# A chunked RWKV recurrence: products on half arrays instead of block diagonals, old state added on TensorE, two groups half a step apart

## The chip, the cores and the metric

The kernel runs on one core of one Trainium2 chip. The metric is the device time of one execution in microseconds, the median of several runs. All times below come from the timed runs or from one execution taken by the hardware profiler.

## What is computed

A trunk of two layers over 1024 tokens and width 1024: attention and feed-forward, then an RWKV-7 time mix and feed-forward, all in 32-bit floats. The part at issue is the time mix's recurrence for 16 heads of 64, cut here to what matters:

```python
def wkv7_scan(r, decay, k, v, a_vec, b_vec):
    def step(state, inp):
        r_t, w_t, k_t, v_t, a_t, b_t = inp
        sa = jnp.einsum('bhvk,bhk->bhv', state, a_t)
        state = state * w_t[:, :, None, :] + sa[..., None] * b_t[:, :, None, :] + v_t[..., None] * k_t[:, :, None, :]
        return state, jnp.einsum('bhvk,bhk->bhv', state, r_t)
    _, ys = lax.scan(step, state0, xs)
...
    y = wkv7_scan(rh, decay, kh, vh, -kk, kk * ah)
    y = ((y - mean) * lax.rsqrt(var + LNX_EPS)).reshape(bsz, s, dm) * lnx_w + lnx_b
    y = y + bonus.reshape(bsz, s, dm)
    out = (y.astype(h.dtype) * g) @ w_o
```

## The kernel before

The time steps are taken in 16 chunks of 64 tokens, a chunk being a step `c` of the stage `rwkv_scan`. Everything that doesn't depend on the state is made beforehand by `rwkv_dense` and kept in DRAM: per chunk and head, the matrices `nk` (64x64), `ar` (64x128: one half for the right side, one for the output), `km` and `bm` (64x128: one half for the new state, one for the output), and `u`, the inverse of a triangular matrix. Its diagonal blocks of 32 come from `solve`: 62 VectorE operations (L1076, L1077) for a quarter of the heads and chunks at a time, four times. The off-diagonal block of each 64 is made in `inverse`, for a pair of chunks at a time, by two rounds of eight TensorE products (L1406, L1414), with ScalarE copies from u (L1410), of tb (L1411) and back into u (L1417) between and behind them.

The 16 heads lie as 8 head pairs, one head in each half of the 128 partitions, and these in 2 groups of 4. A step does for each group, in `step`:

- `o1` = nk x vb + ar x S (L1477, L1479, L1483). Two heads of a pair share one product; the right operands `vb` and `S` are block diagonals, zero outside, so that 128 columns are streamed for two times 64 useful ones.
- `rb`, the right side, copied out of PSUM into a block diagonal in two halves, one by ScalarE (L1485), one by VectorE (L1486).
- `z` = u x rb (L1489), copied into the block diagonal `sb` in the same way (L1490, L1491).
- `o2` = km x vb + bm x sb (L1493, L1495): new state and output.
- the state: VectorE adds the old state (`se`, L1503), GpSimd multiplies by the decay `el` (`S`, L1504).
- the output `y`: a ScalarE copy of the rest of o1 (L1510) and a VectorE addition (L1511).

After each odd step the pair of chunks is finished (`finish`): mean on VectorE (L1520, L1521), y - mean on GpSimd (L1522), the square on ScalarE (L1524), variance on VectorE (L1525, L181), the power -1/2 (L183) and two products on GpSimd (L1530, L1531), y + vn on VectorE (L1532), transposes on TensorE (L1537), the gate on VectorE (`yg`, L1540), and a split into two parts for the output projection: a ScalarE cast and a VectorE subtraction (L154).

Loads of a step (`load`) go through SyncE's queue into two sets of buffers, by the parity of the step; `u` is loaded for two steps at once (`load2`). Each engine works through its own rows strictly in the order in which the built program has them, and waits on semaphores for the others. The order of the rows is made when the program is built, by a scheduler that goes by its own estimates of the durations; `chained` fixes the order of some matmuls. The last solve is called as `last()` after the second step.

Of the kernel before, what the change touches and what calls it, by code (L numbers as in the profile page):

```python
# [1028 lines left out]
def rwkv_dense(t, hp, sv, hT, first):  # L1029
# [73 lines left out]
    for q in range(2):  # L1103
# [156 lines left out]
        for c in range(NK):  # L1260
# [55 lines left out]

            tm = [tp.tile([P, 8, P], F32, name="tm", tag="tm") for _ in range(2)]
            for e in range(2):
                rows = slice(e * 64, e * 64 + 64)
                na = tp.tile([P, 8, 64], F32, name="na", tag="na")  # L1320
                for h in range(2):
                    h4 = slice(h * 4, h * 4 + 4)
                    ps = pg.tile([P, 4, P], F32, name="pg", tag="pg")
                    for i in range(4):
                        pe.matmul(ps[:, i], bk[rows, h * 4 + i].rearrange("p x t -> p (x t)"),  # L1325
                                  ar[rows, h * 4 + i].rearrange("p y t -> p (y t)"), start=True, stop=True)
                    mask = lambda y: mg[:, y * 64:y * 64 + 64].unsqueeze(1).broadcast_to([P, 4, 64])
                    ve.tensor_tensor(na[:, h4], ps[:, :, 0:64], mask(0), MUL)
                    ve.tensor_tensor(tm[e][:, h4, 64:], ps[:, :, 64:], mask(1), MUL)
                nc.sync.dma_start(d["n"][q, e, :, c], na[0:64])  # L1330
                nc.sync.dma_start(d["nk"][cs, rows, c].rearrange("c p t -> p c t"), na[64:])

            for h in range(2):
                h4 = slice(h * 4, h * 4 + 4)
                ps = pg.tile([P, 4, P], F32, name="pg", tag="pg")
                for i in range(4):
                    pe.transpose(ps[:, i], bk[:, h * 4 + i].rearrange("p x t -> p (x t)"), t.ident)
                for e in range(2):
                    ac.copy(tm[e][:, h4, 0:64], ps[:, :, e * 64:e * 64 + 64])
# [21 lines left out]
class Scan:  # L1361


    def __init__(self, t, d):
# [5 lines left out]
        self.zs = [(self.zeroed(lp, "nk0", 1, 2, 5, 64)[0], self.zeroed(lp, "vb0", 1, 2, 8, 64)[0])]  # L1370
# [11 lines left out]

    def more(self, sp):
        self.pools.append(sp)
        self.zs.append((self.zeroed(sp, "nk1", 1, 2, 5, 64)[0], self.zeroed(sp, "vb1", 1, 2, 8, 64)[0]))
# [33 lines left out]
    def load(self, c):  # L1419
        nc, d, pool = self.t.nc, self.d, self.pools[c % 2]  # L1420
        r = []
        for n in ("ar", "bm", "km"):
            x = pool.tile([P, 8, P], F32, name=n, tag=n)
            nc.sync.dma_start(x, d[n][c])
            r.append(x)
        nk, vb = self.zs[c % 2]
        nc.sync.dma_start(nk[:, :, 0:4], d["nk"][c].rearrange("p (g k) t -> p g k t", g=2))
        for e in range(2):
            nc.sync.dma_start(vb[self.half[e], e], d["v"][e, c * 64:c * 64 + 64])
        self.tiles[c % 2] = r + [nk, vb]  # L1430


def rwkv_scan(t, d, ld, sv, last):
# [11 lines left out]
    p1, pz, p2, pq, pg = (pool(n, b, space=PSUM) for n, b in (("sp1", 2), ("spz", 2), ("sp2", 2), ("spq", 1), ("spg", 1)))  # L1445
    Ss, rbs, sbs = (ld.zeroed(sp, n, m, 4, P) for n, m in (("S", 4), ("rb", 2), ("sb", 2)))
    ld.more(sp)
    lo, hi = half = [slice(0, 64), slice(64, P)]

    def chained(seq):  # L1450

        prev = None
        for f in seq:
            ins = f()
            if prev is not None:
                tc.add_manual_dep(ins.ins, prev.ins.name,
                                  mybir.DependencyInfo(mybir.DependencyClass.NoSync, mybir.DependencyReason.DATA), reason="order")
            prev = ins
# [9 lines left out]
    def step(c, two, ar, bm, km, nk, vb):  # L1468
        cc = c % 2
        us, y = two  # L1470
        for grp in range(2):
            pairs = list(enumerate(range(4 * grp, 4 * grp + 4)))
            S, S2, rb, sb = Ss[2 * grp + cc], Ss[2 * grp + 1 - cc], rbs[grp], sbs[grp]
            o1 = p1.tile([P, 4, P], F32, name="o1", tag="o1")
            nkf = nk[:, grp].rearrange("p k t -> p (k t)")

            seq = [lambda: pe.matmul(o1[:, 3], nkf[:, 192:320], vb[:, :, 4 * grp + 3], start=True, stop=c == 0, skip_group_check=True)]  # L1477
            for i, k in pairs[:3]:
                seq.append(lambda i=i, k=k: pe.matmul(o1[lo, i], nk[:, grp, i], vb[:, :, k], start=False, stop=c == 0,  # L1479
                                                      skip_group_check=True))  # L1480
            if c:
                for i, k in pairs:
                    seq.append(lambda i=i, k=k: pe.matmul(o1[:, i], ar[:, k], S[:, i], start=False, stop=True, skip_group_check=True))  # L1483
            chained(seq)
            ac.copy(rb[lo, :, 0:64], o1[lo, :, 0:64])  # L1485
            ve.tensor_copy(rb[hi, :, 64:], o1[lo, :, 64:])  # L1486
            z = pz.tile([64, 4, P], F32, name="z", tag="z")
            for i, k in pairs:
                pe.matmul(z[:, i], us[cc][:, k], rb[:, i], start=True, stop=True)  # L1489
            ac.copy(sb[lo, :, 0:64], z[:, :, 0:64])  # L1490
            ve.tensor_copy(sb[hi, :, 64:], z[:, :, 64:])  # L1491
            o2 = p2.tile([P, 4, P], F32, name="o2", tag="o2")
            chained([lambda i=i, k=k: pe.matmul(o2[:, i], km[:, k], vb[:, :, k], start=i == 0, stop=False, skip_group_check=True)  # L1493
                     for i, k in pairs] +
                    [lambda i=i, k=k: pe.matmul(o2[:, i], bm[:, k], sb[:, i], start=False, stop=True, skip_group_check=True)  # L1495
                     for i, k in pairs])
            if c + 1 < NC:
                se = tp.tile([P, 4, 64], F32, name=f"se{grp}", tag=f"se{grp}", bufs=1)
                for e in range(2):
                    es_ = slice(e * 64, e * 64 + 64)  # L1500
                    el = d["el"][half[e], 4 * grp:4 * grp + 4, c:c + 1].broadcast_to([64, 4, 64])
                    if c:
                        ve.tensor_tensor(se[half[e]], o2[lo, :, es_], S[half[e], :, es_], ADD)  # L1503
                        po.tensor_tensor(S2[half[e], :, es_], se[half[e]], el, MUL)  # L1504
                    else:
                        ve.tensor_tensor(S2[half[e], :, es_], o2[lo, :, es_], el, MUL)
            ys = y[half[cc], grp * H:(grp + 1) * H].rearrange("p (k x) -> p k x", x=P)
            if c:
                y1 = tp.tile([P, 4, P], F32, name="y1", tag="y1")[half[cc]]
                ac.copy(y1, o1[hi])  # L1510
                ve.tensor_tensor(ys, o2[hi], y1, ADD)  # L1511
            else:
                ve.tensor_copy(ys, o2[hi])
# [36 lines left out]
    prev = None  # L1550
    for c in range(NC):
        here = two
        if c == 0:
# [6 lines left out]
        step(c, here, *ld.tiles[c % 2])  # L1560
# [17 lines left out]

# [53 lines left out]
```

## Time and profile before

| | before |
|---|---|
| median of 3 runs | 2867.52 us (2865.66 to 2872.91) |
| profiled execution | 2867.93 us, its span 2866.2 us |
| mean granted TensorE clock | 0.958 |
| window 1965 to 2098 us (chunk 6 to the end of the recurrence) | 133 us |
| TensorE matmuls / weight loads busy there | 115.5 / 101.3 us |
| VectorE / ScalarE / GpSimd busy there | 86.1 / 55.1 / 79.0 us |
| granted clock, DMA share, rate there | 0.97, 0.70, 196 GB/s |

How to read the rows in the next parts. A row of the windows has the stretch, its length, the busy time of PE (matmul), PEld (weight load), DVE (VectorE), ACT (ScalarE) and POOL (GpSimd), then granted clock, DMA share and GB/s. A row of the groups has line, engine, operation, out<-in, shapes and count, then busy time and mean ns of one, then the engine's idle time just before them and what ended it. Rows of the chain of waits and of the timeline begin with the start time and the duration; SPq is SyncE's queue. Matmul ends are modelled. A matmul in 32-bit floats is two records.

### The profile page before, as it was taken

To read this page: it belongs to the slowest core of one execution; us is meant where nothing else is said; L and a number is where in the kernel's file an instruction comes from. 1 tells how busy PE (TensorE), PEld (TensorE's weight loads), DVE (VectorE), ACT (ScalarE), POOL (GpSimd) and SP (SyncE) were. 2 spreads that over 40 slices of the span, in tenths; PEclk is the share of its full clock that TensorE was granted. 3 is DMA by queue.
4 is the path that set the end of the run, shared out by engine and by line. 5 is a ranking of instruction groups with operands and counts; after the bars stand their busy time and mean duration, and the time that the engine had idled before them with its cause. 6 is when DMAs were issued, how large, how long until landed. Compare 5 with 4: busy or idle time off the path is not lost. (4 is left out here: it accounts for less than half of the span.)

```text
span 2866.2 us, 38024 instructions
## 1 busy us (share of the span) xinstructions
PE 2674.2 (93%) x13302; PEld 2135.3 (75%) x13302; DVE 1789.1 (62%) x3017; ACT 1204.6 (42%) x2377; POOL 1099.7 (38%) x830
## 2 busy tenths in 40 slices
PE   8999997799999999998899889888899999999998
PEld 6777775577888877786577667777787888887776
DVE  4555555457444437798667888767676544444988
ACT  3445444234333334355544454434334433333334
POOL 1221211136443424545444433334643534431644
PEclk9999997799999999999999999789999999999999
DMA  4111111452222227462446366787743222225654
GB/s 138 38 45 46 45 51 46 150 191 78 83 82 78 85 94 263 151 207 78 154 138 166 98 212 163 195 216 208 208 162 129 89 89 77 85 70 184 217 155 162
DMA packets 301536, 367.18 MB, mean 128 GB/s; under 512 B 101000, under 2 KB 175112, under 8 KB 301344
## 3 DMA queue, kind: packets, MB, share of 16 engines
q1 hardware_dynamic: 296560, 351.08, 39.5%
q10 hardware_dynamic: 4496, 12.62, 1.1%
q8 instruction: 105, 1.72, 0.3%
q0 software_dynamic: 288, 1.05, 0.1%
q14 instruction: 87, 0.71, 0.1%
HBM read 268.98 MB, written 95.68 MB: 127 GB/s over the span
## 5 line engine op out<-in xcount | busy, mean ns | idle before, releaser
L910 PE MATMUL pd<-ws,as 128*128 128x512 f32 x1848 | 435.7, 397 | 19.9 <-DVE ws L154 18.8
L910 PEld LDWEIGHTS pd<-ws,as 128*128 128x128 f32 x1848 | 353.5, 192 | 100.0 <-DVE ws L154 23.9
L762 PE MATMUL y<-t,cw 128*128 128x512 f32 x1584 | 370.2, 389 | 0.0
L762 PEld LDWEIGHTS y<-t,cw 128*128 128x128 f32 x1584 | 297.3, 188 | 62.4
L154 DVE TENSOR_TENSOR cw<-raw,cw 128x512 fp32r<-128x512 f32 x264 | 214.5, 815 | 197.2 <-ACT cw L154 195.9
L154 ACT CAST cw<-raw 128x512 fp32r<-128x512 f32 x264 | 163.4, 621 | 242.5 <-PE z L762 102.3
L154 ACT CAST wh<-raw 128x512 fp32r<-128x512 f32 (+1 forms) x154 | 119.8, 780 | 202.5 <-PE mm L174 58.4
L154 DVE TENSOR_TENSOR wl<-raw,wh 128x512 fp32r<-128x512 f32 (+1 forms) x146 | 144.0, 988 | 95.2 <-ACT wh L154 94.9
L771 POOL TENSOR_TENSOR c<-c 128x512 f32<-128x512 f32 x66 | 111.4, 1688 | 188.1 <-DVE c L778 137.0
L173 PE MATMUL mm<-hx,wh 128*128 128x512 f32 x384 | 163.3, 425 | 0.0
L766 ACT COPY sn<-y 128x512 f32<-128x512 f32 x132 | 77.0, 588 | 196.4 <-PE y L762 193.1
L175 PE MATMUL mm<-hx,wl 128*128 128x512 f32 x384 | 152.3, 397 | 0.0
L174 PE MATMUL mm<-hx,wh 128*128 128x512 f32 x384 | 151.6, 395 | 0.0
L762 PE MATMUL z<-b,cw 128*128 128x512 f32 x576 | 141.6, 396 | 6.6 <-DVE tx L708 6.6
L257 POOL TENSOR_TENSOR ry<-ry,S 128x512 f32<-128x512 f32 x40 | 52.0, 1301 | 222.5 <-DVE ry L256 198.0
L154 ACT CAST as<-raw 128x512 fp32r<-128x512 f32 x110 | 68.3, 621 | 157.4 <-PE pd L910 82.3
L762 PEld LDWEIGHTS z<-b,cw 128*128 128x128 f32 x576 | 110.2, 192 | 30.8 <-issue 7.0
L762 PE MATMUL y<-b,cw 128*128 128x512 f32 x528 | 129.0, 394 | 0.0
L762 PE MATMUL z<-t,cw 128*128 128x512 f32 x528 | 123.3, 389 | 0.0
L804 POOL TENSOR_TENSOR raw<-s,raw 128x512 f32<-128x512 f32 x44 | 59.9, 1362 | 152.8 <-DVE cw L154 152.6
L762 PE MATMUL x<-b,cw 128*128 128x512 f32 x480 | 117.4, 400 | 0.0
L154 DVE TENSOR_TENSOR as<-raw,as 128x512 fp32r<-128x512 f32 x110 | 100.0, 909 | 27.4 <-ACT as L154 27.3
(469 smaller groups left out, 6122.5 us busy)
## 6 DMA issues: line engine op xcount, KB each, us to landing
raw<-act SPq DMA_DIRECT2D x132, 256.0 KB, 3.5
raw<-in_wd SPq DMA_DIRECT2D x132, 256.0 KB, 3.3
raw<-in_wg SPq DMA_DIRECT2D x88, 256.0 KB, 2.9
raw<-in_wu SPq DMA_DIRECT2D x88, 256.0 KB, 2.5
act<-c SPq DMA_DIRECT2D x88, 256.0 KB, 2.0
raw<-in_wrk SPq DMA_DIRECT2D x32, 512.0 KB, 4.6
raw<-in_win SPq DMA_DIRECT2D x24, 512.0 KB, 3.3
raw<-in_wout SPq DMA_DIRECT2D x32, 256.0 KB, 3.8
```

Source lines behind the costliest of these rows:

```text
L154: return self.nc.scalar.copy(hi, src), (eng or self.nc.vector).tensor_tensor(lo, src, hi.bitcast(F32), SUB)
L173: seen(mm(ps, lh, rh, start=start, stop=False))
L174: seen(mm(ps, lh, rl, start=False, stop=False))
L175: seen(mm(ps, ll, rh, start=False, stop=stop))
L257: nc.gpsimd.tensor_tensor(y, y, self.S[:, s], MUL)
L762: seen(pe.matmul(ps, w[:, x, s], bs[:, k, y], start=start and k == j == 0, stop=k == 3 and j == 2, skip_group_check=True))
L766: ac.copy(s, ps)
L771: po.tensor_tensor(g, g, u, MUL)
L804: po.tensor_tensor(a11, s, a11, SUB)
L910: pe(ps[b], s[:, x, t], w[:, y], start=first and i == 0, stop=f == N - 1 and i == 2, skip_group_check=True)
```

## The change

Each head gets its own products. A head's operands lie in one half of the partitions, so that a product with 64x64 weights uses a quarter of TensorE's array, and one with 64 rows and 128 columns of weights a half; the heads of a pair alternate. Per group and step these are 8 products nk x v and 8 ar x S into the first half of one PSUM tile `xz`, 16 for the old state (the identity times S into the state's half of o2, and the output half of ar times S into the other), 8 km x v, 8 u x rb into the second half of `xz`, and 8 bm x sb. `o2` is now two PSUM tiles, one for each head of a pair. The block diagonals, their zeroing, `se`, `y1` and GpSimd's part are gone: `rb` is one ScalarE copy, `sb` one VectorE copy, the state two VectorE products with the decay, the output two ScalarE copies. In DRAM, the halves of `km` and `bm` of the second head are swapped. The loads come in the order ar, nk, vb, km, bm, with the same bytes. All products of the recurrence are chained in the order of the code, and the two groups, now generators, are advanced in turn, so that group 1 is half a step behind group 0.

The core of the diff:

```diff
@@ load
-        for n in ("ar", "bm", "km"):
-            x = pool.tile([P, 8, P], F32, name=n, tag=n)
-            nc.sync.dma_start(x, d[n][c])
...
+        ar = pool.tile([P, 8, P], F32, name="ar", tag="ar")
+        nc.sync.dma_start(ar, d["ar"][c])
+        nk, vb = (pool.tile([P, 8, 64], F32, name=n, tag=n) for n in ("nk", "vb"))
...
@@ rwkv_scan
-    p1, pz, p2, pq, pg = (pool(n, b, space=PSUM) for n, b in (("sp1", 2), ("spz", 2), ("sp2", 2), ("spq", 1), ("spg", 1)))
-    Ss, rbs, sbs = (ld.zeroed(sp, n, m, 4, P) for n, m in (("S", 4), ("rb", 2), ("sb", 2)))
+    p1, p2, pq, pg = (pool(n, b, space=PSUM) for n, b in (("sp1", 2), ("sp2", 4), ("spq", 1), ("spg", 1)))
...
+    def mm(*x, **k):
+        ins = pe.matmul(*x, **k, skip_group_check=True)
+        if order:
+            t.after(ins, order.pop())
+        order.append(ins)
...
-    def step(c, two, ar, bm, km, nk, vb):
...
+    def group(g):
+        Ss, S = [sp.tile([P, 4, 64], F32, name=f"S{g}{i}") for i in range(2)], None
+        both = [(i, e, half[e]) for i in range(4) for e in range(2)]
+        k0 = 4 * g
+        for c in range(NC):
+            us, y = here
+            ar, bm, km, nk, vb = ld.tiles[c % 2]
+            xz = p1.tile([P, 2, 4, 64], F32, name="xz", tag="xz")
+            for i, e, r in both:
+                mm(xz[r, 0, i], nk[r, k0 + i], vb[r, k0 + i], start=i == 0, stop=c == 0)
+            if c:
+                for i, e, r in both:
+                    mm(xz[r, 0, i], ar[r, k0 + i, 0:64], S[r, i], start=False, stop=True)
+            rb, sb = (tp.tile([P, 4, 64], F32, name=n, tag=f"{n}{g}", bufs=1) for n in ("rb", "sb"))
+            ac.copy(rb, xz[:, 0])
+            yield
+            o2 = [p2.tile([P, 4, 64], F32, name="o2", tag="o2") for _ in range(2)]
+            if c:
+                for i, e, r in both:
+                    mm(o2[e][r, i], t.ident[r, r], S[r, i], start=i == 0, stop=False)
+                    mm(o2[e][half[1 - e], i], ar[r, k0 + i, 64:], S[r, i], start=i == 0, stop=False)
+            for i, e, r in both:
+                mm(o2[e][:, i], km[r, k0 + i], vb[r, k0 + i], start=c == i == 0, stop=False)
+            for i, e, r in both:
+                mm(xz[r, 1, i], us[c % 2][r, k0 + i], rb[r, i], start=True, stop=True)
+            ve.tensor_copy(sb, xz[:, 1])
+            yield
+            for i, e, r in both:
+                mm(o2[e][:, i], bm[r, k0 + i], sb[r, i], start=False, stop=True)
+            if c + 1 < NC:
+                S = Ss[c % 2]
+                for e, r in enumerate(half):
+                    ve.tensor_tensor(S[r], o2[e][r], d["el"][r, k0:k0 + 4, c:c + 1].broadcast_to([64, 4, 64]), MUL)
+            ys = y[half[c % 2], g * H:(g + 1) * H].rearrange("p (k e v) -> p e k v", e=2, v=64)
+            for e in range(2):
+                ac.copy(ys[:, e], o2[e][half[1 - e]])
+            yield
...
+    groups = [group(g) for g in range(2)]
     for c in range(NC):
         here = two
+        next(groups[0])
+        if c:
+            next(groups[1])
...
-        step(c, here, *ld.tiles[c % 2])
+        next(groups[0])
+        next(groups[1])
+        next(groups[0])
+        next(groups[1])
+        if c + 1 == NC:
+            next(groups[1])
```

The order of the rows around the change moves too. Lines of the changed kernel differ by a few from those of the kernel before; names carry numbers of their buffers.

VectorE, where a pair of chunks ends in the middle of the stage, before (`rb0`, `rb1`, `sb1`, `se0`, `se1` are those of the groups; `mean`, `var` and `rs_v` belong to the finish of the pair that has just ended):

```order
L1520 TENSOR_REDUCE mean_17012<-y_16450 128x16
L154 TENSOR_TENSOR o_15926<-yg_16792,o_15926 128x4x128
L1521 TENSOR_SCALAR mean_17012<-mean_17012 128x16
L1486 COPY rb1_15504<-o1_16859 64x4x64
L1540 SCALAR_TENSOR_TENSOR yg_16804<-pg_16799,vec_62,gt_16572 128x128 x4
L1511 TENSOR_TENSOR y_16691<-o2_16842,y1_16856 64x512
L154 TENSOR_TENSOR o_15927<-yg_16804,o_15927 128x4x128
L1491 COPY sb1_15508<-z_16870 64x4x64
L1486 COPY rb0_15503<-o1_16942 64x4x64
L1525 TENSOR_REDUCE var_17013<-sqy_17017 128x16
L1503 TENSOR_TENSOR se1_16886<-o2_16877,S2_15497 64x256 x2
L1511 TENSOR_TENSOR y_16691<-o2_16877,y1_16891 64x512
```

VectorE at the same place of the changed kernel (`S00` and `S10` are the states of groups 0 and 1 behind the even step; the first `sb` is that of group 0, the second that of group 1):

```order
L154 TENSOR_TENSOR o_16062<-yg_17772,o_16062 128x4x128
L1507 TENSOR_REDUCE mean_18112<-y_17252 128x16
L1508 TENSOR_SCALAR mean_18112<-mean_18112 128x16
L1512 TENSOR_REDUCE var_18113<-sqy_18117 128x16
L181 TENSOR_SCALAR rs_v_18120<-var_18113 128x16
L1489 COPY sb_17801<-xz_17783 128x256
L1496 TENSOR_TENSOR S00_15521<-o2_17826,el_10639 64x256
L1496 TENSOR_TENSOR S00_15521<-o2_17827,el_10639 64x256
L1519 TENSOR_TENSOR y_17252<-y_17252,vn_17779 128x1024
L1489 COPY sb_17879<-xz_17861 128x256
```

Before, the mean and the variance of a finish had other rows between them (eight in this piece), among them copies of rb and sb. Now they follow each other, the first sb copy of the next pair of steps stands behind the variance, and its second sb copy behind `y + vn`.

ScalarE at the same place, before (`u20` is the copy out of the freshly loaded u, `sqy` the finish's square):

```order
L1490 COPY sb0_15507<-z_16835 64x4x64
L1410 COPY u20_13714<-u_16894 32x8x32 x4
L1417 COPY u_16894<-pq_16919 32x8x32 x4
L154 CAST o_15926<-yg_16792 128x4x128
L1485 COPY rb1_15504<-o1_16859 64x4x64
L1510 COPY y1_16891<-o1_16859 64x512
L1411 COPY tb0_13712<-pq_17143 32x8x32 x4
L154 CAST o_15927<-yg_16804 128x4x128
L1490 COPY sb1_15508<-z_16870 64x4x64
L1485 COPY rb0_15503<-o1_16942 64x4x64
L1524 ACTIVATE sqy_17017<-y_16450 128x1024
```

And ScalarE there in the changed kernel (the first `y` row is that of group 0 in the odd step, the two behind the second cast are those of group 1, with which the pair's y is complete):

```order
L1499 COPY y_17252<-o2_17638 64x4x64
L154 CAST o_16061<-yg_17760 128x4x128
L1478 COPY rb_17800<-xz_17783 128x256
L1406 COPY u20_13714<-u_17960 32x8x32 x4
L154 CAST o_16062<-yg_17772 128x4x128
L1499 COPY y_17252<-o2_17704 64x4x64
L1499 COPY y_17252<-o2_17705 64x4x64
L1511 ACTIVATE sqy_18117<-y_17252 128x1024
L1478 COPY rb_17878<-xz_17861 128x256
```

The copies from u, which wait for a load, now stand between the even step's first rb copy and the cast, and ahead of the y copies, of the square and of the second rb copy.

SyncE at the end of the dense stage, before (`n` is what the last solve reads; `n_d`, `bm_d` and `km_d` are in DRAM):

```order
L1342 DMA bm_d_10633<-tm_15403 64x8x128
L1343 DMA km_d_10634<-tm_15403 64x8x128
L1429 DMA vb00_13718<-v_d_10630 64x512
L1565 DMA bo_15729<-bon_d_10631 128x8x16
L1424 DMA bm_15650<-bm_d_10633 128x1024
L1070 DMA n_15731<-n_d_10636 32x32x32 x4
```

And SyncE there in the changed kernel:

```order
L1070 DMA n_15798<-n_d_10636 32x32x32 x2
L1331 DMA n_d_10636<-na_15402 64x512
L1332 DMA nk_d_10635<-na_15402 64x8x64
L1343 DMA bm_d_10633<-tm_15400 64x8x128
L1344 DMA km_d_10634<-tm_15400 64x8x128
L1343 DMA bm_d_10633<-tm_15401 64x8x128
L1344 DMA km_d_10634<-tm_15401 64x8x128
L1070 DMA n_15798<-n_d_10636 32x32x32 x2
```

Two of the solve's four loads have moved ahead of the last stores, and three other issues no longer stand between those stores and the rest. In VectorE's rows, the 62 operations of this solve, which before began behind the sb copies of step 1 and reached to step 5, now begin ahead of the first sb copy of step 0 and end after that of group 0 in step 1.

More of the change, by code (lines that the diff above doesn't have):

```diff
@@ L1328, in rwkv_dense @@
                     ve.tensor_tensor(na[:, h4], ps[:, :, 0:64], mask(0), MUL)
-                    ve.tensor_tensor(tm[e][:, h4, 64:], ps[:, :, 64:], mask(1), MUL)
+                    ve.tensor_tensor(tm[e][:, h4, 64 - 64 * e:P - 64 * e], ps[:, :, 64:], mask(1), MUL)
                 nc.sync.dma_start(d["n"][q, e, :, c], na[0:64])
@@ L1338, in rwkv_dense @@
                 for e in range(2):
-                    ac.copy(tm[e][:, h4, 0:64], ps[:, :, e * 64:e * 64 + 64])
+                    ac.copy(tm[e][:, h4, e * 64:e * 64 + 64], ps[:, :, e * 64:e * 64 + 64])
             for e in range(2):
@@ L1369, in __init__ @@
         self.nb, self.ub, self.tb, self.u2 = (self.zeroed(lp, n, 1, 8, 64)[0] for n in ("nb", "ub", "tb", "u2"))
-        self.zs = [(self.zeroed(lp, "nk0", 1, 2, 5, 64)[0], self.zeroed(lp, "vb0", 1, 2, 8, 64)[0])]
         self.pools, self.us, self.tiles = [lp], [None, None], [None, None]
@@ L1381, in begin @@
         self.load(0)
-    def more(self, sp):
-        self.pools.append(sp)
-        self.zs.append((self.zeroed(sp, "nk1", 1, 2, 5, 64)[0], self.zeroed(sp, "vb1", 1, 2, 8, 64)[0]))
     def load2(self, g):
@@ L1420, in load @@
         nc, d, pool = self.t.nc, self.d, self.pools[c % 2]
-        r = []
-        for n in ("ar", "bm", "km"):
-            x = pool.tile([P, 8, P], F32, name=n, tag=n)
-            nc.sync.dma_start(x, d[n][c])
-            r.append(x)
-        nk, vb = self.zs[c % 2]
-        nc.sync.dma_start(nk[:, :, 0:4], d["nk"][c].rearrange("p (g k) t -> p g k t", g=2))
-        for e in range(2):
-            nc.sync.dma_start(vb[self.half[e], e], d["v"][e, c * 64:c * 64 + 64])
-        self.tiles[c % 2] = r + [nk, vb]
+        ar = pool.tile([P, 8, P], F32, name="ar", tag="ar")
+        nc.sync.dma_start(ar, d["ar"][c])
+        nk, vb = (pool.tile([P, 8, 64], F32, name=n, tag=n) for n in ("nk", "vb"))
+        nc.sync.dma_start(nk, d["nk"][c])
+        for e in range(2):
+            nc.sync.dma_start(vb[self.half[e]], d["v"][e, c * 64:c * 64 + 64])
+        km, bm = (pool.tile([P, 8, P], F32, name=n, tag=n) for n in ("km", "bm"))
+        nc.sync.dma_start(km, d["km"][c])
+        nc.sync.dma_start(bm, d["bm"][c])
+        self.tiles[c % 2] = ar, bm, km, nk, vb
 def rwkv_scan(t, d, ld, sv, last):
@@ L1444, in rwkv_scan @@
     sp, tp = pool("ss", 1), pool("st", 2)
-    p1, pz, p2, pq, pg = (pool(n, b, space=PSUM) for n, b in (("sp1", 2), ("spz", 2), ("sp2", 2), ("spq", 1), ("spg", 1)))
-    Ss, rbs, sbs = (ld.zeroed(sp, n, m, 4, P) for n, m in (("S", 4), ("rb", 2), ("sb", 2)))
-    ld.more(sp)
+    p1, p2, pq, pg = (pool(n, b, space=PSUM) for n, b in (("sp1", 2), ("sp2", 4), ("spq", 1), ("spg", 1)))
+    ld.pools.append(sp)
     lo, hi = half = [slice(0, 64), slice(64, P)]
[L1450 to L1458, printed above, removed]
+    order = []
+    def mm(*x, **k):
[3 more added lines that the diff above has]
+        order.append(ins)
     def load3(g):
@@ L1466, in load3 @@
         return vn, gt
-    def step(c, two, ar, bm, km, nk, vb):
[L1469 to L1480, printed above, removed]
-            if c:
[L1482 to L1496, printed above, removed]
-            if c + 1 < NC:
[L1498 to L1513, printed above, removed]
```

## The prediction, on record before the run

> **What bounds the kernel now.** I read the page first, then the table of windows to find the stage that the change touches, the groups of that stage, its waits, and the chain of waits in order of time. The recurrence over the 16 chunks runs from about 1865 to 2098 us, and it is not a stage of full TensorE: in the window 1965 to 2098 (chunk 6 to the end) TensorE is busy in 115.5 of 133 us, VectorE in 86.1, GpSimd in 79.0, and the DMA engines in 0.70 of the time.
>
> ```profile
> 1965.00:2098.00 133.00, 115.53 (x927) 101.32 (x926) 86.11 (x171) 55.08 (x123) 78.97 (x63) 0.97 0.70 196
> L1486 DVE COPY rb<-o 64x256 f32<-64x256 f32 x19 | 7.9, 416 | 15.1 <-ACT rb L1485 14.8
> L1504 POOL TENSOR_TENSOR S<-se,el 64x256 f32<-64x256 f32 x38 | 25.7, 675 | 26.1 <-DVE se L1503 24.5
> L1491 DVE COPY sb<-z 64x256 f32<-64x256 f32 x20 | 8.3, 417 | 5.5 <-ACT sb L1490 5.1
> L1485 ACT COPY rb<-o 64x256 f32<-64x256 f32 x19 | 7.0, 366 | 31.9 <-PE o L1483 31.7
> L1410 ACT COPY u<-u 32x256 f32<-32x256 f32 x16 | 6.4, 402 | 15.3 <-DMA u<-u_d 15.1
> L1411 ACT COPY tb<-pq 32x256 f32<-32x256 f32 x16 | 5.8, 362 | 2.7 <-PE pq L1406 2.5
> L154 ACT CAST o<-yg 128x512 fp32r<-128x512 f32 x12 | 7.3, 618 | 1.4 <-DVE yg L1540 1.3
> ```
>
> Nineteen copies of rb at two a step are 9.5 steps in 133 us, so a step takes 14.0 us and a pair of steps 28.0. The reader is to see two things: the pieces of work are small (0.4 us copies, 0.7 us state products), and engines mostly wait for one another. One wait to keep in mind is ScalarE's for the load of u.
>
> ```profile
> 1979.28 1.12 PE pq L1406 x16
> ...
> 1981.48 0.89 PE o L1495 x8
> 1982.38 1.02 PE z L1489 x8
> 1983.39 0.93 PE pq L1414 x16
> 1984.74 0.80 PE o L1479 x6
> ...
> 1994.33 5.52 DMA u<-u_d
> ...
> 2020.40 1.10 PE z L1489 x8
> 2021.56 4.35 DMA u<-u_d
> ...
> 2044.31 1.10 PE z L1489 x8
> 2045.47 6.51 DMA u<-u_d
> ...
> 2096.01 2.12 PE o L1495 x16
> ```
>
> In this chain of waits, each matmul is two records. Records that stream 128 columns follow each other every 0.111 us (0.89 over 8), those that stream 64 every 0.058 us (0.93 over 16), and a burst that begins a new shape loses about 0.13 us (1.02 against 0.89; 0.80 for six against 0.67). A load of u starts when the last z that read the buffer has ended, and lands 4.4 to 6.5 us later, 5.5 in the mean. The last product of the recurrence ends at 2098.1.
>
> **TensorE's part of the change.** Per group and step, 20 matmuls (40 records) become 56 (112 records) on half or quarter arrays. Whether halves run at the same time is seen elsewhere in this trace:
>
> ```profile
> 202.53 1.09 PE L490 MATMUL pv<-pT,vt 128*64 128x128 f32 x16
> 205.16 1.13 PE L454 MATMUL sc<-kT,q 64*128 64x256 f32 x8
> 1851.03 2.05 PE L1325 MATMUL pg<-ar,bk 64*128 64x128 f32 x16
> ```
>
> L490 alternates the column halves and takes 1.09 us for sixteen records; L1325, which stays in one row half, takes 2.05 for sixteen of the same length. L454 alternates row halves and takes 1.13 for eight records of 256 columns, which one after another at 0.111 per 128 would be 1.78. So halves overlap. For each of the three products with 64x64 weights (the two into xz, and U with rb) I take 8 x 0.058 = 0.46 us; one after another they would be 0.93. The products with the identity and ar (32 records) lie between 0.46 (four at a time) and 1.86 (none): I take 0.93, pairs, which is what the two rows show. The products with km and bm have 64 moving columns but weights 128 columns wide: between 0.46 and 1.78, I take 0.89, the pace of L454's pairs at 128. With four changes of shape at 0.13, a half-step is 1.39 + 0.93 + 1.78 + 0.52 = 4.6 us, a step 9.2, and with the inverse ((1.12 + 0.93)/2) and the finish's transposes (eight records and two bursts in two steps, 0.6) 10.9 us. If TensorE set the pace, a step would fall from 14.0 to 10.9.
>
> **Why I don't think it sets the pace.** VectorE and ScalarE work through their rows in order, and the rows shown above put the whole finish of a pair (mean, variance, scaling) between the last state product of that pair and the first copies of sb of the next one, back to back. In the kernel before, other work stands between the same links, and they cost almost nothing:
>
> ```profile
> DVE var L1525 <- ACT sqy L1524: 2.9, 1, 2.9
> DVE y L1532 <- POOL y L1531: 1.0, 1, 1.0
> ```
>
> (3.9 us in 133.) What the links take is seen undisturbed at the end of the stage, in the finish of the last pair:
>
> ```profile
> 2098.90 1.22 DVE L1520 TENSOR_REDUCE mean<-y 128x16 f32<-128x1024 f32 x1
> 2101.17 0.17 DVE L1521 TENSOR_SCALAR mean<-mean 128x16 f32<-128x16 f32 x1
> 2101.48 1.91 POOL L1522 TENSOR_TENSOR y<-y,mean 128x1024 f32<-128x1024 f32 x1 [1.95 <-DVE mean L1521]
> 2103.42 1.06 ACT L1524 ACTIVATE sqy<-y 128x1024 f32<-128x1024 f32 x1 [1.86 <-POOL y L1522]
> 2104.51 1.22 DVE L1525 TENSOR_REDUCE var<-sqy 128x16 f32<-128x1024 f32 x1 [0.58 <-ACT sqy L1524]
> 2106.25 0.17 DVE L181 TENSOR_SCALAR rs_v<-var 128x16 f32<-128x16 f32 x1
> 2106.50 2.90 POOL L183 TENSOR_TENSOR rs_r<-rs_v,mhalf 128x16 f32<-128x16 f32 x1 [3.11 <-DVE rs_v L181]
> 2109.47 1.91 POOL L1530 TENSOR_TENSOR y<-y,rs_r 128x1024 f32<-128x1024 f32 x1
> L1531 POOL TENSOR_TENSOR y<-y,lw 128x1024 f32<-128x1024 f32 x5 | 11.8, 2358 | 0.4
> 2114.67 1.21 DVE L1532 TENSOR_TENSOR y<-y,vn 128x1024 f32<-128x1024 f32 x1
> ```
>
> One pair of steps in the changed kernel, from the end of the copy sb (odd step, group 1) round to the same copy:
>
> - A, until the mean may start: ScalarE's four copies from u stand ahead of the cast and of the y copies that the mean needs. The last U product ended 0.77 us earlier (0.35 to VectorE, 0.42 the copy), the load lands 5.5 after that, then four copies of 0.402, a cast of 0.62, two y copies of 0.73 together and 0.3 of hand-overs: 8.0 us. Bounds: 5.3 if u is never late (VectorE's own yg, split and state rows), 9.0 at the longest load.
> - B, the finish from mean to y+vn, which stands ahead of sb (even step, group 1): 1.22 + 0.17 + 1.91 + 1.06 + 1.22 + 0.17 + 2.90 + 1.91 + 2.36 + 1.21 = 14.1, with nine hand-overs 14.6 us. Only one sb copy and one pair of state products fit into its waits.
> - C, three half-steps: sb 0.52; bm 1.0; then 3.5 until the inverse's second half may start (0.25 to VectorE, state 0.84, y copies 0.8, four tb copies of 0.362, hand-overs), that half 1.05, the second half of km 0.57, U 0.58, to VectorE and copy 0.77, bm 1.1, identity, ar and km 2.06, U 0.58, copy 0.77: 12.5 us.
>
> Together 35.1 us for a pair, against 28.0 now. VectorE's saving (the second halves of rb and the additions se and y are gone) and GpSimd's (38 products of 0.675 gone) fall into these waits and bring nothing. The copies of rb and sb in one piece do take 0.8 us out of the round trip; that is in C.
>
> **The clock.** By A and B TensorE then waits about 9 us for the first sb of a pair (mean to rs_v, behind the late y copies) and 4 us for the second (y+vn). After a wait of 2.3 us the trace shows a burst at about half pace:
>
> ```profile
> 1972.66 1.82 PE L1489 MATMUL z<-rb,u 128*64 128x128 f32 x8 [0.45 <-DVE rb L1486]
> ```
>
> (1.82 against 1.02.) Behind the first wait slow products are covered by the finish; behind the second they lie in C. Between 0 and 2 us a pair, I take 1. The Trainium skill (TensorE: Matmul & The Clock Gate, "What's actually happening") says that the array falls to half clock after an idle window of about 3.4 us and recovers after a busy one; by it the second wait would cost an estimated 1.7 us a pair, 12 us in all where I take 7.
>
> **The start.** The fourth triangular solve (62 VectorE operations) is spread over chunks 2 to 6 now, and takes longer beside GpSimd's work than the third did:
>
> ```profile
> 1895.11 0.19 DVE L1076 TENSOR_TENSOR sw<-ub,n 128x31 f32<-128x31 f32 x1 [4.13 <-DMA n<-n_d]
> 1883.89 1.04 SPq L1429 DMA_DIRECT2D vb<-v_d  x1
> 1887.04 4.22 SPq L1070 DMA_DIRECT2D n<-n_d  x4
> L1077 DVE TENSOR_TENSOR ub<-ub,sw 128x31 f32<-128x31 f32 (+15 forms) x31 | 12.7, 411 | 0.6
> L1076 DVE TENSOR_TENSOR sw<-ub,n 128x31 f32<-128x31 f32 (+15 forms) x31 | 11.9, 384 | 1.3 <-DMA n<-n_d 0.9
> ```
>
> In the new order it starts before the first sb copy and ends with one and a half steps done. Three other issues no longer stand ahead of its loads (1887.04 - 1883.89 = 3.2 us), so it starts at about 1892, takes 24.6 (12.7 + 11.9) and carries 3.8 of sb and state rows: 1920.4, and sb (step 1, group 1) ends at 1920.8. From there seven pairs remain: 7 x 35.1 = 245.7, 2 for the last products, 7 for the clock: 2175.5 instead of 2098.1, that is +77 us. What follows the stage is unchanged. The profiled execution took 2867.93 us (the median of the runs is 2867.52), so 2945 us.
>
> **The rivals.**
> - Faster: TensorE sets the pace. Then 1920.8 + 14 x 10.9 + 2 = 2075, 23 us less, 2845. For it speak the falling work of VectorE and GpSimd, and that a 9 us cut of A and B is all that is needed: the change is not slower from a pair of about 26 us down. Against it: GpSimd's links have no slack to give, L1531's five in the stage average 2.36, and the same kind took 1.91 alone; the order of the rows is fixed. 0.07.
> - Halves better than I take them: identity, km and bm all at 0.46. Only C shrinks, by 2 us: 33.1 a pair, +63, 2931. 0.22.
> - The quarter products into xz don't overlap, since both row halves write one bank: no row shows that case, L454 uses two banks. U and the new xz products then cost 0.46 to 0.93 more where they lie in C, about 2 us a pair: 37.1, +91, 2959. The Trainium skill (TensorEngine Tiling (Array Packing), Gotcha 1: PSUM Pressure) states that different row tiles cannot access the same PSUM bank at one time, which is this case; no run here shows it yet. 0.13.
> - The change doesn't do what it says, nothing overlaps: C grows by 6 us, 41.1 a pair, +119, 2987. 0.07.
>
> **How the numbers follow.** My forecast has 0.51; its own range is 2919 (u never late, no clock loss) to 2959. The range of 2900 to 2980 takes in the second and third rival and the bounds of u and the clock, and leaves out the first and the last. A measurement of this kernel can tell about 0.3%, 8.6 us, from no change: faster 0.06, same 0.03, slower 0.91.
>
> **What would show it.** In the profile after, VectorE's variance waits for the square and its y+vn for GpSimd, each some 3 to 5 us in every pair; TensorE's bm products wait for sb; ScalarE's copy from u waits for the DMA; pairs of steps are 35 us apart; the window's DMA share falls to about 0.56 (0.70 x 28.0/35.1). Sixteen 64x64 records should take about 0.5 to 0.6 us. I am wrong if steps come every 11 to 14 us: then something other than the order of VectorE's rows decides.

## The result and the profile after

| | before | after |
|---|---|---|
| median of four runs each, side by side | 2870.22 us (2865.66 to 2875.29) | 2954.24 us (2947.41 to 2957.35) |
| profiled execution, its span | 2867.93, 2866.2 us | 2955.12, 2953.3 us |
| mean granted clock | 0.958 | 0.932 |

The changed kernel is slower: after over before is 1.0292, with a 95% interval of 1.0273 to 1.031. The first view is the table of windows for the recurrence after, from 10 us behind the first sb (odd step, group 1) to just before the last; the columns are those explained above.

```profile
1925.00:2178.00 253.00, 175.20 (x3216) 160.45 (x3216) 82.20 (x174) 69.29 (x170) 74.76 (x34) 0.72 0.47 143
```

TensorE is busy in 69% of the stage (87% before) at a granted clock of 0.72 (0.97 before), and the DMA share fell from 0.70 to 0.47. Per step VectorE, ScalarE and GpSimd are busy for less than before. TensorE is busy for 12.9 us a step (181.0 over 14 steps, 1915.1 to 2178.7 us) where it was 12.2 (115.5 over 9.5), at the lower clock. What grew most is waiting. The waits of the same window (who waits, for whom, us in all, times, longest):

```profile
PEld o L1449 <- DVE sb L1489: 84.1, 14, 15.4
PE o L1449 <- DVE sb L1489: 81.9, 14, 15.3
...
ACT u L1406 <- DMA u<-u_d: 36.3, 6, 10.1
```

All of TensorE's larger waits are for sb copies, fourteen in all: two in each pair of steps. Why sb is late is seen in VectorE's rows of one pair, in order of time (rows of yg, split and state left out):

```profile
2029.22 0.42 DVE L1489 COPY sb<-xz 128x256 f32<-128x256 f32 x1 [1.47 <-issue]
...
2040.91 1.22 DVE L1507 TENSOR_REDUCE mean<-y 128x16 f32<-128x1024 f32 x1
2042.16 0.17 DVE L1508 TENSOR_SCALAR mean<-mean 128x16 f32<-128x16 f32 x1
2045.50 1.22 DVE L1512 TENSOR_REDUCE var<-sqy 128x16 f32<-128x1024 f32 x1 [3.16 <-ACT sqy L1511]
2046.76 0.17 DVE L181 TENSOR_SCALAR rs_v<-var 128x16 f32<-128x16 f32 x1
2046.96 0.42 DVE L1489 COPY sb<-xz 128x256 f32<-128x256 f32 x1
...
2054.36 1.23 DVE L1519 TENSOR_TENSOR y<-y,vn 128x1024 f32<-128x1024 f32 x1 [4.03 <-POOL y L1518]
2055.61 0.42 DVE L1489 COPY sb<-xz 128x256 f32<-128x256 f32 x1
2062.39 0.42 DVE L1489 COPY sb<-xz 128x256 f32<-128x256 f32 x1 [4.28 <-issue]
2066.63 0.42 DVE L1489 COPY sb<-xz 128x256 f32<-128x256 f32 x1 [1.47 <-issue]
```

From 2040.91 to 2055.59 VectorE does one sb copy between the links of the finish: the first copy of the next pair has to let mean and variance by, the second y+vn. From sb to sb this pair took 37.4 us. The chain of waits shows the other half of the story, from the end of this pair into the next:

```profile
2063.22 2.70 PE o L1449 x64
2065.92 0.64 PE xz L1449 x16
...
2066.76 0.59 SPq L1422
...
2067.40 0.58 SPq L1424
...
2068.09 6.64 DMA u<-u_d
2074.75 0.40 ACT u L1406
...
2076.42 0.62 ACT o L154
2077.06 0.37 ACT y L1499
2077.45 0.37 ACT y L1499
2077.84 1.23 DVE mean L1507
...
2083.90 0.44 DVE sb L1489
...
2084.38 4.93 PE o L1449 x64
```

The load of u has to wait for the last U product (it ends at 2066.56), stands behind two other issues in SyncE's queue until 2068.09, and only when it has landed may ScalarE go on to the y copies that the mean needs. The state's products then wait until 2084.38, and take 4.93 us for 64 records, where the same products took 2.70 at 2063.22. That is the clock:

```profile
2072.00:2076.00 4.00, 1.63 (x48) 1.35 (x42) 0.00 (x0) 1.22 (x4) 0.00 (x0) 1.00 1.14 327
2076.00:2084.00 8.00, 0.00 (x0) 0.00 (x0) 3.58 (x6) 3.05 (x6) 1.96 (x2) 0.50 0.15 56
2084.00:2096.00 12.00, 10.66 (x138) 10.01 (x139) 3.66 (x7) 1.54 (x5) 7.10 (x3) 0.50 0.21 65
2096.00:2103.00 7.00, 7.00 (x94) 6.41 (x93) 0.00 (x0) 3.19 (x9) 1.90 (x1) 0.50 1.05 263
2103.00:2108.00 5.00, 5.00 (x118) 4.50 (x116) 1.69 (x4) 1.10 (x3) 0.00 (x0) 0.97 0.44 101
```

The granted clock (third number from the right) is 0.50 behind the wait and stays there for 19 us of nearly unbroken work (one pause of 0.9 us at 2092, for the second sb). At full clock the new products are as fast as hoped; TensorE's rows of the same step once the clock is back:

```profile
2104.05 1.11 PE L1449 MATMUL o<-sb,bm 64*128 64x64 f32 x16
...
2105.71 1.11 PE L1449 MATMUL o<-vb,km 64*128 64x64 f32 x16
2106.75 0.68 PE L1449 MATMUL xz<-rb,u 64*64 64x64 f32 x16
...
2107.95 0.68 PE L1449 MATMUL xz<-vb,nk 64*64 64x64 f32 x16
2108.46 0.63 PE L1449 MATMUL xz<-S,ar 64*64 64x64 f32 x16
```

From start to start, bm with the 32 records of the old state behind it takes 1.66, km 1.04, U 0.61, nk 0.51 and ar 0.57: 4.4 us for a half-step.

### The profile page after: what moved, and what is told of

Read it like the earlier page. It is cut to its first block, busy times and chain, and to the rows that moved or that the text cites. A ratio compares the mean times of both kernels' runs of the same rounds, so it can differ in the third digit from the quotient of the medians.

```text
span 2953.3 us, 42217 instructions
## 1 busy us (share of the span) xinstructions
PE 2684.8 (91%) x15526; PEld 2152.5 (73%) x15526; DVE 1735.2 (59%) x2953; ACT 1197.1 (41%) x2379; POOL 1054.0 (36%) x762
## 5 line engine op out<-in xcount | busy, mean ns | idle before, releaser
L154 DVE TENSOR_TENSOR cw<-raw,cw 128x512 fp32r<-128x512 f32 x264 | 214.3, 814 | 198.1 <-ACT cw L154 197.0
L154 ACT CAST cw<-raw 128x512 fp32r<-128x512 f32 x264 | 163.3, 621 | 243.1 <-PE z L762 102.5
L154 ACT CAST wh<-raw 128x512 fp32r<-128x512 f32 (+1 forms) x154 | 119.6, 779 | 204.6 <-PE mm L174 58.4
L154 DVE TENSOR_TENSOR wl<-raw,wh 128x512 fp32r<-128x512 f32 (+1 forms) x146 | 144.1, 990 | 98.8 <-ACT wh L154 98.5
L1449 PE MATMUL o<-sb,bm 64*128 64x64 f32 x512 | 48.1, 339 | 94.7 <-DVE sb L1489 94.7
L154 ACT CAST as<-raw 128x512 fp32r<-128x512 f32 x110 | 68.2, 620 | 158.1 <-PE pd L910 85.5
L762 PEld LDWEIGHTS y<-b,cw 128*128 128x128 f32 x528 | 98.8, 187 | 22.7
```

The lines of the kernel that those rows point to most:

```text
L154: return self.nc.scalar.copy(hi, src), (eng or self.nc.vector).tensor_tensor(lo, src, hi.bitcast(F32), SUB)
L762: seen(pe.matmul(ps, w[:, x, s], bs[:, k, y], start=start and k == j == 0, stop=k == 3 and j == 2, skip_group_check=True))
L1449: ins = pe.matmul(*x, **k, skip_group_check=True)
```

## The experiments

Two theories stood. **Order**: the products are faster, but VectorE's and ScalarE's rows put the whole finish and the late copy of u into the loop from sb to sb. **TensorE**: the products on half arrays are themselves slow or hinder each other. All ratios below are to the kernel before, run on the same chip beside them (2869.28 to 2870.41 us); differences in us from the changed kernel go by its 2954.24, measured beside 2870.22.

### One cause at a time

`u2`: two buffers for each u, so that its load need not wait for the last product that reads the old one.

```diff
-        u = self.pools[g % 2].tile([P, 8, 2, 64], F32, name="u", tag="u")
+        u = self.pools[g % 2].tile([P, 8, 2, 64], F32, name="u", tag="u", bufs=2)
```

> Only edit: two buffers for each of the two u tiles, so that a load of u needn't wait for the last U product. Theory 'order' (the fixed order of VectorE's and ScalarE's rows puts the finish and the late u on the path of every pair): from the copy sb (odd step, group 1) to the mean falls from about 10.5 us to about 5.3, six times, the finish from mean to y+vn stays at 14.7: about 30 us less than the changed kernel, 2925 us. Rival 'TensorE' (the many small products and the lower clock are the cost): ScalarE's wait goes, the time stays within 9 us of 2954.

Measured: 2918.73 us (2914.93 to 2925.7), ratio 1.0173 (1.0155 to 1.0192), some 35 us better than the changed kernel, near the 2925 of the theory of the order and far from the rival's. The rows of one pair:

```profile
1979.47 0.42 DVE L1489 COPY sb<-xz 128x256 f32<-128x256 f32 x1 [2.23 <-issue]
1985.01 1.22 DVE L1507 TENSOR_REDUCE mean<-y 128x16 f32<-128x1024 f32 x1
...
1998.45 1.23 DVE L1519 TENSOR_TENSOR y<-y,vn 128x1024 f32<-128x1024 f32 x1 [4.04 <-POOL y L1518]
```

From sb's end to the mean it is 5.1 us now (11.3 in the pair shown above); from the mean to the end of y+vn still 14.67. Pairs take 31.3 to 34.1 us instead of 37.4 to 40.9.

`nofin`: the norm and the bonus of the finish are left out (L1507 to L1519; y goes to the transposes as it is).

> The changed kernel without the norm of the finish: mean, y - mean, square, variance, power, the two products and y+vn are left out (and with them the bonus), transposes, gate and split stay; the output isn't the reference's. Products, their number and their shapes are unchanged. Theory 'order': sb no longer stands behind the finish, what is left of a pair is TensorE's 21 us, 2 to 3 us of the late u and 1 to 2 us at the inverse: about 25 instead of 38, seven pairs: 2855 to 2875 us. Rival 'TensorE' (the small products and their clock cost the time): 2930 us or more.

Measured: 2897.81 us (2894.65 to 2900.97), ratio 1.0091 (1.0061 to 1.012): between both theories' numbers, a miss. Pairs take 29.6 to 31.5 us, the granted clock from 1925 to 2075 us is 0.79, and what is left in them is the other cause:

```profile
ACT u L1406 <- DMA u<-u_d: 34.2, 5, 12.6
```

(five waits in 150 us.) So one cause gone leaves the other, with its own waits and low clock: this run could not tell the theories apart. The next one does.

`nofin_u2`: both edits together.

> The changed kernel with the norm and the bonus of the finish left out (y goes to the transposes as it is) and two buffers for u. Theory of the order (the finish links and the late u copy together are the loss): a pair then has no finish and no late u, about 22 to 25 us, 7 pairs of them where now 39: 2954 minus 7 x 14 to 17 = 2835 to 2856. Rival, TensorE is slow by itself on halves (each pair over 30 us with all waits of the order gone): 2885 or more.

Measured: 2839.85 us (2838.2 to 2841.49), ratio 0.9893 (0.9867 to 0.9919), as the theory of the order has it. Alone the two edits brought 35 and 56 us, together 114. The window of the recurrence:

```profile
1925.00:2075.00 150.00, 143.76 (x3268) 130.34 (x3267) 58.40 (x150) 63.62 (x165) 0.00 (x0) 1.00 0.82 233
```

TensorE is busy 96% at a granted clock of 1.00; steady pairs take 21.3 to 21.8 us. The new products are thus no hindrance: freed of the order they take 10.7 us a step, where a step took 14.0 before. This run also leaves out the work of the finish; `spread2` below keeps it.

`before_gated`: the opposite test. The kernel before, with its own products and loads, but VectorE's rows in the order of the changed kernel: group 0's sb of an even step behind rs_v, group 1's behind y+vn.

```diff
-            ve.tensor_copy(sb[hi, :, 64:], z[:, :, 64:])
+            x = ve.tensor_copy(sb[hi, :, 64:], z[:, :, 64:])
+            if gate is not None:
+                t.after(x, gate[grp])
```

> The kernel before, with only the order that the changed kernel has: VectorE's sb copy of group 0 in an even step stands behind the variance of the pair before, that of group 1 behind its y+vn. Products, copies and loads are those of before. Theory 'order': a pair can't be shorter than the finish (14.6 us) and about one and a half steps (18 to 20): 32 to 35 us instead of 28, seven times: 2895 to 2920 us. Rival 'TensorE': the order of the finish isn't what costs, 2870 us within 9.

Measured: 2933.46 us (2930.39 to 2937.68), ratio 1.0223 (1.0208 to 1.0238). The order alone, without any new product, costs 63 us, more than expected. Its pairs, measured from one y+vn to the next, are 35.6 to 40 us long (28.0 without the gate), and the granted clock in its window 1925 to 2075 falls to 0.85 (0.97 without the gate):

```profile
1925.00:2075.00 150.00, 113.35 (x802) 99.85 (x802) 79.61 (x168) 49.82 (x111) 62.28 (x51) 0.85 0.61 167
```

```profile
1965.43 1.23 DVE L1537 TENSOR_TENSOR y<-y,vn 128x1024 f32<-128x1024 f32 x1 [1.80 <-POOL y L1536]
1966.68 0.42 DVE L1491 COPY sb<-z 64x256 f32<-64x256 f32 x1
...
2005.39 1.23 DVE L1537 TENSOR_TENSOR y<-y,vn 128x1024 f32<-128x1024 f32 x1
```

For this the finish up to y+vn is also called ahead of the step, so that rows of the other engines move with it. TensorE's waits put down to sb are 10.3 us from 1925 to 2115 (0.5 before, 1925 to 2098); the rest of the loss is in its other waits and in the lower clock. The 63 us are thus the price of the whole order, not of the two sb copies by themselves.

### Giving the finish another order

`spread`: the links of the finish are spread over the next two steps, each behind a copy of rb or sb (mean behind sb of group 0, square behind rb of group 1, variance and y+vn behind sb of group 1 in turn, the gate after the state), with a third buffer for y.

```diff
-        ve.tensor_reduce(mean, h(y), AX.X, ADD)
+        behind(ve.tensor_reduce(mean, h(y), AX.X, ADD), sbs[0])
...
-        ve.tensor_tensor(pairs(y), pairs(y), vn, ADD)
+        yield
+        behind(ve.tensor_tensor(pairs(y), pairs(y), vn, ADD), sbs[1])
```

> The finish of a pair is spread over the next pair of steps by order dependencies: mean behind sb (even step, group 0), square behind rb (even, 1), variance behind sb (even, 1), y+vn behind sb (odd, 1), transposes and gate in the step after, half behind each group's state. Three y buffers. Nothing is left out. Theory 'order': no sb copy stands behind the finish any more, TensorE sets the pace at 10.5 to 11.5 us a step, and the late u costs up to 5 us a pair: 2845 to 2885 us, faster than or near the kernel before. Rival 'TensorE': the products, their number and their clock are unchanged, so 2920 us or more. Rival 'u load': the mean no longer waits for it, but if the copies from u are what holds the pair, pairs stay at 35 us or more.

Measured: 2908.91 us (2906.56 to 2909.48, and one execution of 6900.43 for which no trace shows a cause and which the ratio leaves out), ratio 1.0131 (1.0111 to 1.0152): a miss. `spread_u2` adds the second buffers for u.

> Both edits together. Theory 'order': steps of 10.5 to 11.5 us from the end of the solve, recurrence ends at 2065 to 2080 us instead of 2180: 2840 to 2855 us, which would beat both kernels. The granted clock in the stage rises from 0.72 to above 0.9, since TensorE no longer waits. Rival 'TensorE': 2900 us or more. Rival 'transfers': a step can't be shorter than its transfers, 9.8 us at a share of 1.0 and 12 us at 0.8: 2855 to 2870 us with a DMA share above 0.8.

Measured: 2892.57 us (2889.68 to 2892.91), ratio 1.0077 (1.0062 to 1.0092): a miss too. The waits of its window 1925 to 2110 say why:

```profile
POOL vn L1523 <- DMA vn<-v_d: 44.0, 3, 15.4
DVE o L154 <- ACT o L154: 40.5, 12, 9.5
ACT sqy L1517 <- POOL y L1514: 38.7, 6, 9.9
```

A new wait took the place of the old one. GpSimd's product vn x bo stood ahead of y - mean in its queue and waited for the load of vn (three times, by the first row); the square waited for GpSimd, ScalarE's cast for the square, VectorE's split (L154) for the cast, and sb stood behind the split. Spreading VectorE's links isn't enough while one of GpSimd's stands in the wrong place.

`spread2` mends this: vn x bo behind GpSimd's other links, three buffers for vn and gt, the mean behind the state of group 1, gate and split behind sb, the inverse in two parts, the first at the end of the even step.

```diff
+        x = po.tensor_tensor(y, y, lw, MUL)
+        behind(po.tensor_tensor(vn, vn, bo[:, g].rearrange("p (k e) -> p k e", e=2).unsqueeze(3).broadcast_to([P, 8, 2, 64]), MUL), x)
...
-    def pair(g):
-        ld.inverse(g, pq)
+    def pair(g):
+        inv = ld.inverse(g, pq, order)
+        next(inv)
+        yield
+        next(inv)
```

> The spread finish, with what held the first version's pairs at 27 to 34 us taken out: the product vn x bo stands behind the other GpSimd links instead of ahead of them (it waited for its load), three buffers for vn and gt, the mean directly behind the state of group 1, gate and split behind sb, and the inverse in two parts, the first at the end of the even step. Theory 'order': pairs of 22 to 24 us from 1915 us on: the recurrence ends at 2070 to 2085, 2845 to 2860 us. Rival 'transfers': a pair needs 20 us of transfers at a share of 1.0 and about 24 at 0.82: 2855 to 2875 us with a share above 0.8. Rival 'TensorE': 2890 us or more.

Measured: 2851.64 us (2850.62 to 2854.1), ratio 0.9931 (0.9914 to 0.9949), as expected, 102.6 us better than the changed kernel and faster than the kernel before. Its window, and one pair of VectorE's rows:

```profile
1925.00:2075.00 150.00, 142.92 (x3240) 130.31 (x3238) 78.75 (x172) 68.95 (x169) 75.33 (x35) 0.96 0.80 236
```

```profile
1988.69 0.42 DVE L1500 COPY sb<-xz 128x256 f32<-128x256 f32 x1 [1.48 <-PE xz L1460]
1989.14 1.22 DVE L1533 TENSOR_TENSOR y<-y,vn 128x1024 f32<-128x1024 f32 x1
1991.88 1.22 DVE L1518 TENSOR_REDUCE mean<-y 128x16 f32<-128x1024 f32 x1 [0.43 <-ACT y L1510]
...
1998.37 1.22 DVE L1525 TENSOR_REDUCE var<-sqy 128x16 f32<-128x1024 f32 x1
...
2009.98 0.42 DVE L1500 COPY sb<-xz 128x256 f32<-128x256 f32 x1 [1.49 <-PE xz L1460]
```

The same links take as long as ever, but none holds up sb any more: sb waits for its own product (`PE xz`), and a pair takes 21.3 us. TensorE, busy in 95% of the window, is the bound now. How much each of these edits brought was not measured one by one.

`spread3` adds one thing: the fourth solve is spread over steps 1 to 3, ten of its operations behind each sb.

> As the run before, and the fourth solve is spread over steps 1 to 3, ten VectorE operations behind each sb copy, instead of standing in one piece at the start. Theory 'order': steps 1 to 3 take about 11 us each from about 1890 on, instead of one and a half steps in the 27 us of the solve: some 8 to 15 us less than the run before: 2832 to 2850 us, faster than the kernel before. Rival: the copies out of the dense stage or the loads hold the first steps, then no gain over the run before.

Measured: 2849.63 us (2847.26 to 2853.48), ratio 0.992 (0.9899 to 0.9942). The 2 us to `spread2` are less than the runs differ among themselves; the expected 8 to 15 didn't come.

### Do halves run at the same time, and what does half a step bring

`after_runs`: the changed kernel, only the order of the heads in each product changed: the four of one row half, then the four of the other, so that neighbours don't alternate. `spread2_runs` is the same edit in `spread2`, where TensorE is the bound.

```diff
-        both = [(i, e, half[e]) for i in range(4) for e in range(2)]
+        both = [(i, e, half[e]) for e in range(2) for i in range(4)]
```

> The changed kernel with one line changed: the products go through all four pairs of the first row half, then of the second, so that neighbours no longer use different row halves and TensorE's half-step grows from 4.4 us to about 8. Theory 'order': only what lies between y+vn and the last sb of a pair grows, some 5 to 6 us a pair, less where a longer busy stretch raises the clock: 2975 to 3000 us. Rival 'TensorE': every half-step counts, 28 x 3.7 us: 3050 us or more.

> The version with the spread finish (2851.6, TensorE busy in 95% of its stage, pairs of steps 21.4 us apart), its only edit the list of heads: the four products of one row half first, then the four of the other, so that neighbours do not lie in different halves. If neighbours in different halves run at one time and TensorE is the bound there: the products of a pair of steps, four half-steps of 4.4 us, take up to twice as long, pairs of 30 to 38 us, 13 to 15 of the half pairs slower: 2915 to 2965. Rival, the halves bring nothing (the gain comes from the removed vector work alone): no change, 2850 to 2856.

Measured: `after_runs` 3026.59 us (3014.36 to 3038.81), ratio 1.0539 (1.0483 to 1.0596), between the two numbers, which settles neither theory; `spread2_runs` 2953.06 us (2952.11 to 2954.01), ratio 1.0288 (1.0261 to 1.0314), 101 us slower than `spread2`, as expected. Alternating halves is what the speed of the new products rests on. But the edit works in two ways, as three stretches of `spread2_runs` show:

```profile
2005.00:2009.00 4.00, 4.00 (x91) 3.86 (x90) 2.50 (x4) 0.81 (x3) 0.00 (x0) 1.00 0.72 246
2011.00:2028.00 17.00, 17.00 (x155) 15.52 (x155) 5.52 (x14) 2.68 (x5) 1.80 (x1) 0.50 0.50 162
2031.00:2035.00 4.00, 4.00 (x70) 3.73 (x70) 0.84 (x2) 1.98 (x7) 3.84 (x3) 1.00 0.62 107
```

```profile
2040.37 1.60 PE L1460 MATMUL o<-vb,km 64*128 64x64 f32 x16
2041.90 0.79 PE L1460 MATMUL xz<-rb,u 64*64 64x64 f32 x13
```

At a granted clock of 1.00 a half-step takes 6.0 us (sb to sb) where `spread2` takes 4.25; the km products, for one, take 1.53 from start to start, 1.04 when neighbours alternate. And for long stretches the clock is 0.50 although no idle time of TensorE is recorded. Pairs are 36.4 us in the mean against 21.9.

`spread2_instep`: `spread2` with its two groups in step instead of half a step apart.

```diff
-        if c:
-            next(groups[1])
+        next(groups[1])
...
-        if c + 1 == NC:
-            next(groups[1])
```

> The version with the spread finish, but its two groups in step instead of half a step apart (group 1 is advanced one stage earlier in the first step and no more at the end). If half a step apart is what hides the copies of rb and sb behind the other group's products: TensorE waits for a copy and its hand-overs two times a step, about 0.8 us each, so 3 us or more a pair, 24 to 27 us where it was 21.4: 2875 to 2895. Rival, the chained order of the matmuls hides them either way: within 0.3% of 2851.6, 2843 to 2860.

Measured: 2851.6 us (2848.88 to 2852.53), ratio 0.9932 (0.9912 to 0.9952), the same time as `spread2`: the rival's number. Half a step apart brings nothing here; that part of the change is not what makes `spread2` faster. In the changed kernel itself it wasn't tried.

## Why the prediction was right, point by point

The direction and its cause held: the order of VectorE's and ScalarE's rows decides, and the faster products fall into its waits. Freed of it, the same products give 2851.64; VectorE's order, put into the kernel before, costs 63 us there, where the change costs 84. That the rest comes from the copies of u and y on ScalarE fits `u2`, but wasn't tried in the kernel before. The 2955.12 us of the profiled execution are 10 above the 2945. That they are so near is in part luck: A, B and what follows the stage are 20.6 us longer than predicted, the start and C 10.7 us shorter. The terms, all from sb's end to sb's end over seven pairs:

| term | predicted | measured |
|---|---|---|
| first sb (step 1, group 1) ends | 1920.8 | 1915.1 |
| A, seven times | 7 x 8.0 = 56.0 | 71.5: 13.9, then 9.8 to 11.3, last 5.1 |
| B, seven times | 7 x 14.6 = 102.2 | 7 x 14.67 = 102.7 |
| C with the clock, seven times | 7 x (12.5 + 1) = 94.5 | 89.5: 9.9 to 15.6 |
| what follows: mean of the last pair to the end of the span | unchanged (767.3) | 771.9 |

- **A was mis-sized**: u was taken to land 5.5 us after the last U product; in the chain above it lands 8.2 after (1.5 until it leaves SyncE's queue, 6.6 for the load). That is the 2.7 us by which this pair's 10.8 exceed the 8.0. Five pairs in the middle took 10.5 in the mean, beyond the upper bound of 9.0. In the first pair the load of u stood behind the solve's stores in SyncE's queue. The last pair, counted like the others in the prediction, loads no u: 5.1, which is also what `u2` shows, near the lower bound of 5.3.
- **B held to 0.1 us** in every pair. It was added up from single operations and nine hand-overs of one undisturbed finish.
- **C held in the sum, not in its parts.** At a granted clock of 1.00 it takes 9.9 and 11.5 us (with half of the inverse and all of it in its way), less than the 12.5, in part because the old state's 32 records run on four quarters at once and take 0.62, not 0.93. At 0.82, 0.75, 0.65 and 0.64 it takes 13.1, 13.9, 15.4 and 15.6. Against the 11.5, the clock so costs 1.6 to 4.1 us in four of the seven pairs, 12.1 in all, where 1 in each was taken. The prediction had the slow products behind the first wait covered by the finish. But in three of these pairs the clock was still 0.50 from the first wait when y+vn had ended, and in the fourth it fell again at 1980.4 us, 1.7 us behind a pause of 1.2. The Trainium skill (TensorE: Matmul & The Clock Gate, "What's actually happening") has the array back at full speed after a busy window of about 3.4 us. Here it took 7.0 to 19.2 us from the first product behind each of the seven waits of 5.5 to 15.3 us; 19 of them behind the wait of 10.7 shown, 7.3 behind the longest, the first of the stage. The measurement decides: recovery takes longer than that page gives, and no single length fits. That the 12 us worked out by that figure are near the 12.1 doesn't bear it out, since by it each pair would have lost 1.7.
- **The start** was put 6 us too late: the solve began at 1886.3 instead of 1892.
- **What follows** was not unchanged but took 4.6 us more (771.9); why wasn't followed up.
- **The rivals.** By the time alone the 2959 of the third rival are nearer than the 2945; only the rows tell them apart. That the quarter products into xz run one after another because both row halves write one bank is refuted: nk, ar and U take 0.51 to 0.61 us for sixteen records from start to start, the pace of two at a time (0.46 and one change of shape), where one after another they would take 0.93. The Trainium skill's rule (TensorEngine Tiling (Array Packing), Gotcha 1: PSUM Pressure) isn't borne out for products whose outputs lie in different partitions of the bank. That nothing overlaps is refuted by the same rows and by `spread2_runs`. The second rival's 0.46 for identity, km and bm came for none: 0.62, 1.04 and 1.04. That TensorE sets the pace did not come in this kernel, but comes in `spread2`: 10.7 us a step, where the working had 10.9.
- **The signs**: the variance's wait for the square was 3.2 us and y+vn's for GpSimd 4.0 in each pair, as foretold. The DMA share fell to 0.47, more than to 0.56: pairs but the last are 39 us apart, not 35, which by the same working gives 0.50, and in the last 20 us of the window almost nothing is loaded.

## What to carry to other kernels

When a part is made faster, look at what order its neighbours' rows get: a scheduler that goes by its own estimates put a chain over three engines (14.7 us) in front of a copy for which TensorE waited, and an engine in order can't step aside. Add up the loop from one copy to the same copy a period later, along the rows of each engine, not the busy times. To mend it, put each link of the long chain behind the short chain's copies on every engine it touches; with GpSimd's row left as it was (`spread_u2`, which differs from `spread2` in other points too), 41 of the 103 us were lost, and with one buffer for u besides (`spread`), 57.

## What the runs showed of the hardware

- Products on different quarters of the array run at once when neighbours in the queue alternate: 32 records of 64x64 weights with 64 columns in 0.62 us, 16 in 0.51 to 0.61, also where both row halves write one PSUM bank in different partitions. With 128 columns of weights and 64 streamed, sixteen on alternating row halves take 1.04, and 1.53 where they don't alternate.
- Waits of TensorE cost more than their length: after 10.7 us idle the granted clock stayed at 0.50 for 19 us of work, after six other waits of the stage for 7.0 to 19.2 us. A long wait isn't needed: the clock also fell to 0.50 at 1980.4 us with no idle time but a pause of 1.2 us in the 10 us ahead, and in `spread2_runs` it fell to 0.50 for at least 17 us with no idle time recorded at all. Why it fell there is open; the same products in alternating order (`spread2`) kept 0.96 over the window.
- Causes in one loop aren't additive: 35 and 56 us alone, 114 together. With either one left, waits stay and the granted clock from 1925 to 2075 us is 0.76 (`u2`) and 0.79 (`nofin`); with both gone it is 1.00. That the clock is the whole reason wasn't tried.
